# Loading the first chunk of x and the first quarter of w through the hardware DMA queues

## The chip, the cores and the metric

The kernel runs on one core of one Trainium2 chip. A core has a matrix engine (TensorE, PE in the profile, its weight loads PEld), a vector engine (VectorE, DVE), a scalar engine (ScalarE, ACT), a general engine (GpSimd, POOL) and a queue engine (SyncE, SP) that only issues DMAs. Data moves between device memory and the on-chip memory (SBUF) by 16 DMA engines. A DMA is issued on a queue: SyncE and ScalarE issue on hardware queues, which copy without a change of type; GpSimd issues on a software queue, which can cast float32 to bfloat16 on the way. The metric is the device time of the kernel in microseconds (us), the median of several runs.

## The reference

```python
B, S, D = (16, 2048, 1024)
def reference(x, w, decay):            # x [B,S,D], w [D,D], decay [D], float32
    xw = x @ w
    out[:, 0, :] = xw[:, 0, :]
    for t in range(1, S):
        out[:, t, :] = decay[None, :] * out[:, t - 1, :] + xw[:, t, :]
    return out
```

A matrix product, and along the time axis of each of its columns a decayed running sum.

## The kernel before

**Tiling.** The 32768 rows of x are cut into 64 chunks of 512 (`TL`). The inner dimension of 1024 is cut into four quadrants (`NQ`) of 256 (`CQ`); one contraction step k (8 of them, `K`) takes 32 of the 256 rows of each quadrant, so its 128 partitions are 4 blocks of 32. k = 2m + e with m in 0..3 and e in 0..1: the row of w that belongs to quadrant q, index i and step k is 256q + 64m + 2i + e, so the even and the odd rows of w belong to different e. An output block n (8 of them) is 128 columns of the result, laid on 128 partitions; blocks 0 to 3 (h = 0) are the first half of the columns, 4 to 7 (h = 1) the second. Matmuls are in bfloat16: `wsb` holds w, `xt` a chunk of x, transposed so that the contraction lies on partitions; the sum over k is made in PSUM.

**Steady state.** GpSimd's queue loads x casting to bfloat16 (`load`, L105), VectorE transposes blocks of 32 (`turn`, L115), ScalarE puts the pairs apart (`part`, L123), TensorE multiplies (`matmul`, L131), VectorE scans along time (`run` L233, `scan` L213), transposes back (`back`, L283) and SyncE stores (`store`, L306). A tile of the result is an instance of `Tile`.

**Order.** It is written out by hand. `pin` keeps every instruction in the order of the program on its engine. `agenda` is a table from a step to a string of deeds, a letter and a number each; `deeds` says which function a letter calls. Line -99 of the table is the opening, ahead of the first output tile. Each DMA takes one of eight completion semaphores of its kind (hardware or software) in turn, so that the ninth waits until the first of them has landed.

**The opening, which the change touches.** w is loaded in four parts (h, e), the "quarters", into `stage`, memory that later serves as output buffers (`room`); each part is 128 partitions of 4 sets (m) of 512 columns. `load_w` (L321) issues a part as four DMAs of one quadrant each (L323). `settle` (L328, copy on L330) copies one set m of a part to its place in `wsb`. x's first 256 rows come as float32 rows, 128 in each of two DMAs on the queues of SyncE and ScalarE (L341), into `whole`. `gather` (L376) casts them to bfloat16 into `upright`, `erect` (L386) transposes them on TensorE into PSUM (`bed`), `lay` (L393) copies them to `xt`. The second 256 rows come casting by `load_half` on GpSimd's queue and go through `turn` and `part` in halves; `begin(0)` multiplies the first half by all even k, `begin(1)` the second, 256 columns in each matmul. Then come the odd k of the whole chunk, which need w's second part (0, 1), then the first halves of chunk 1 and so on.

`spin` (L350) issues matmuls on a constant tile, whose result is not used; twelve of them open TensorE's work. `spin_on(q)` (L404) makes such matmuls wait for quadrant q of w's first part, by a copy of one of its columns into a `gate` tile. `identity(1)` makes the unit matrix for the transposes on GpSimd (L442, L443). `decays` (L424 to L430) turns the decay rows that SyncE loads on L356 into columns.

The letters of the opening: U = a part of w on GpSimd's queue; M = half a chunk of x on GpSimd's queue; I = unit matrix; H, J = `gather` on VectorE, ScalarE; t = `erect`; O, o = `lay` on ScalarE, VectorE; K = matmuls on the constant; W, w = `settle` of one set on VectorE, ScalarE; q, Q = the same for block 0 and for blocks 1 to 3; n = `begin`; E = a quarter of `turn`; F, G = a quarter of `part` on VectorE, ScalarE; D = `decays`; L = the next load of x. W0 to W3 are the sets of part (0, 0), q4 to W7 those of (0, 1), W8 to w15 those of h = 1.

Of the kernel before, what the change touches and what calls it, by code (L numbers as in the profile page):

```python
# [9 lines left out]
FP32 = mybir.dt.float32  # L10
BF16 = mybir.dt.bfloat16
# [3 lines left out]
def _ap(ap_obj: bass.AP, new_ap, extra_offset=0):  # L15
    return dataclasses.replace(
        ap_obj,
        ap=[list(p) for p in new_ap],
        offset=ap_obj.offset + extra_offset,
    )  # L20
# [5 lines left out]
def kernel(  # L26
# [26 lines left out]
    nc = tc.nc  # L53
    pin = tc.keep_in_program_order
    B, S, D = x.shape
    assert w.shape == (D, D)

    NQ = 4
    P = 32
    CQ = D // NQ  # L60
    K = CQ // P
    M = K // 2
    TL = 512
    NJ = TL // P
    NC = S // TL
    R = K // 2
    CH = D // 2
# [8 lines left out]
    def ring(pool, name, count, shape, dtype=FP32):  # L76
        i = turns[name] = turns.get(name, -1) + 1
        return pool.tile(shape, dtype, name=f"{name}{i % count}")

    def quad(q):  # L80
        return slice(q * P, (q + 1) * P)
# [59 lines left out]
    class Tile:  # L141
# [39 lines left out]
        def copy(self):  # L181
            self.xs = sb.tile([128, 2 * TL], FP32, name=f"xs{self.lot % 3}")[:, 0:self.T]
            parts = self.ps if isinstance(self.ps, tuple) else (self.ps,)
            size = self.T // len(parts)
            for i, ps in enumerate(parts):
                pin(nc.scalar.copy(out=self.xs[:, i * size:(i + 1) * size], in_=ps))  # L186
# [103 lines left out]
    class Outlet:  # L290
# [8 lines left out]
        def store(self, b, t0, j0, j1):  # L299
# [4 lines left out]
            for j in range(j0, j1, nj):  # L304
# [8 lines left out]

    room = [ot_tile(2 * NJ).rearrange("p j c -> p (j c)") for _ in range(2)]
    size = M * CH
    stage = {(0, 0): room[0][:, 0:size // 2].bitcast(BF16),
             (0, 1): room[0][:, size:size * 3 // 2].bitcast(BF16),
             (1, 0): room[1][:, 0:size // 2].bitcast(BF16),
             (1, 1): room[1][:, size // 2:size].bitcast(BF16)}

    def load_w(queues, h, e):  # L321
        for i, q in enumerate((0, 2, 1, 3)):
            pin(queues[i % len(queues)].dma_start(  # L323
                out=stage[h, e][quad(q)].rearrange("p (m d) -> p m d", m=M),
                in_=_ap(w, [[2 * D, P], [2 * P * D, M], [1, CH]],
                        (q * CQ + e) * D + h * CH)))

    def settle(h, e, m, copy):  # L328
        src = stage[h, e][:, m * CH:(m + 1) * CH]
# [4 lines left out]
    spare = ring(psp, "spare", 1, [128, TL])  # L334
    rows = const.tile([128, 2, P], FP32, name="rows")
    touch = const.tile([128, 1], BF16, name="touch")
    H = NJ // 2
    halves = ((0, H), (H, NJ))
    whole = room[1][:, size:2 * size].rearrange("p (u c) -> p u c", u=2)
    for u, queue in enumerate((nc.sync, nc.scalar)):  # L340
        pin(queue.dma_start(out=whole[:, u], in_=_ap(x, [[D, 128], [1, D]], u * 128 * D)))  # L341
    pin(nc.vector.memset(idle, 0.0))  # L342
    pin(nc.vector.memset(rows, 0.0))
    pin(nc.scalar.copy(out=touch, in_=idle[:, 0:1]))

    gates = [const.tile([128, 128], BF16, name=f"gate{q}") for q in range(NQ)]
    for gate in gates:
        pin(nc.vector.memset(gate, 0.0))

    def spin(count, by):  # L350
        for _ in range(count):
            pin(nc.tensor.matmul(out=spare, lhsT=by, rhs=idle, start=True, stop=True))  # L352

    spin(12, idle[:, 0:128])
    for q in range(NQ):
        pin(nc.sync.dma_start(  # L356
            out=rows[q * P:q * P + R],
# [3 lines left out]
    def load_half(i):  # L361
# [6 lines left out]
    seconds = [ps[:, TL:2 * TL] for ps in heads] + [spares[1]]  # L368
    eye = const.tile([128, 128], BF16, name="eye")

    upright = room[0][:, size * 3 // 2:2 * size].bitcast(BF16).rearrange(
        "p (e u m c) -> p e u m c", e=2, u=2, m=M)

    def gather(i, copy):
        e, u = i // 2, i % 2
        pin(copy(out=upright[:, e, u].rearrange("p m (q i) -> p m q i", q=NQ),  # L376
                 in_=whole[:, u].rearrange(
                     "p (q m i e) -> p e m q i", q=NQ, m=M, e=2)[:, e]))

    def bed(e):  # L380
        return seconds[e].bitcast(BF16).rearrange("p (m t) -> p m t", m=M)

    def erect(i):
        e, u = i // 2, i % 2
        for m in range(M):
            pin(nc.tensor.transpose(  # L386
                out=bed(e)[:, m, u * 128:(u + 1) * 128], in_=upright[:, e, u, m], identity=eye))

    def lay(i, copy):
        e, m = i // 2, i % 2 * 2  # L390
        if 0 not in xt_of:
            xt_of[0] = ring(sb, "xt", 5, [128, M, 2, TL], BF16)
        pin(copy(out=xt_of[0][:, m:m + 2, e, 0:H * P], in_=bed(e)[:, m:m + 2]))  # L393

    def begin(i):
        for k in range(0, K, 2):
            for n in range(R):
                if i == 0:
                    matmul(firsts[n], n, k, xt_of[0], 0, H * P)
                else:  # L400
                    matmul(firsts[n], n, k, xt_of[0], H * P, TL, pairs=xw_of[0])

    def spin_on(q):
        pin(nc.scalar.copy(out=gates[q][quad(q), 0:1], in_=stage[0, 0][quad(q), 0:1]))  # L404
        spin(3 if q == 0 else 2, gates[q])

    def load_part(i):
        load_w((nc.gpsimd,), i // 2, i % 2)

    def part_one(i, copy):  # L410
        part(i // 8, copy, i % 4, i % 4 + 1, *halves[i // 4 % 2])
# [106 lines left out]
    def turn_and_load(c):  # L518
# [19 lines left out]
        "E": lambda i: turn(i // 8, *halves[i // 4 % 2], i % 4, i % 4 + 1),  # L538
        "F": lambda i: part_one(i, nc.vector.tensor_copy),
        "G": lambda i: part_one(i, nc.scalar.copy),  # L540
        "K": spin_on,
        "t": erect,
        "H": lambda i: gather(i, nc.vector.tensor_copy),
        "J": lambda i: gather(i, nc.scalar.copy),
# [24 lines left out]
        "L": lambda i: load(*loads.pop(0)) if loads else None,  # L569
    }  # L570
    agenda = {
        -99: "U0 I1 M1 U1 M2 M3 U2 U3 H0 J1 t0 t1 H2 J3 t2 t3 O1 o0 K0 O3 o2 K2 K1 K3 W0 W1 w2 W3 n0 E4 E5 G4 E6 G5 E7 F6 G7 n1 q4 w5 Q4 W6 W7 D E8 E9 G8 E10 G9 E11 F10 G11 E12 L E13 G12 L E14 G13 E15 L F14 G15",
        0: "p0 z0 W8 W9 W10 W11",
        1: "g0",
        2: "L S1 L",
# [191 lines left out]
```

## Time and profile before

| | us |
|---|---|
| median of 3 runs (lowest, highest) | 903.61 (903.51, 903.97) |
| the profiled execution, its own time | 903.72 |
| its span, first to last instruction | 901.9 |
| TensorE busy | 891.2 |
| VectorE busy | 823.5 |
| ScalarE busy | 687.1 |
| GpSimd busy | 657.2 |

The profile is of one execution. The span is shorter than the time by what lies around the program. Busy times are sums over the span; an engine can be busy at something that nobody waits for. The chain of work that ended last is followed back from the last instruction, at each step to what released it; when it is read in order of time, a row is start, length, what. A row of the timeline is start, length, engine, line, operation, what is written and from what, how many; in brackets the idle time before it and what ended that. A row of a stretch is its two ends, its length, the busy time and number of instructions of TensorE, its weight loads, VectorE, ScalarE and GpSimd, the granted clock, the mean busy share of the 16 DMA engines and what they wrote in GB/s. A row of a DMA queue is its kind, packets, MB written, and the time of its packets as a share of 16 engines' time. TensorE's granted clock stands at 1.0 in every slice. All times in the text are from the start of the span.

### The profile page before, as it was taken

The page shows a single profiled execution, that of the slowest core. Times are in us where ns is not written, and L with a number is a line of the kernel's source. Part 1 is how long each engine was busy: PE and PEld are TensorE (multiplying, and loading weights), DVE is VectorE, ACT ScalarE, POOL GpSimd, SP SyncE. Part 2 cuts the span into 40 slices and gives each one's busy share as a digit, 9 for nine tenths or more (in the row PEclk, how much of TensorE's full clock was granted, in tenths as well). Part 3 has the DMA queues.
Part 4 walks back from the last instruction along what each step waited for, and adds up shares of the span by engine and source line. Part 5 has one row for each costly group of instructions (what it writes and reads, how often), then busy time and mean ns, then how long its engine had stood idle before and what let it go on. Part 6 is the DMA issues. An engine that isn't in the chain of part 4 may idle for free.

```text
span 901.9 us, 12229 instructions
## 1 busy us (share of the span) xinstructions
PE 891.2 (99%) x4131; PEld 411.9 (46%) x4213; DVE 823.5 (91%) x636; ACT 687.1 (76%) x962; POOL 657.2 (73%) x757
## 2 busy tenths in 40 slices
PE   8999999999999999999999999999999999999998
PEld 5544444444444444444444444444444444444444
DVE  4999998989999999999998999999999999999998
ACT  4889867778877877878778778777787787787743
POOL 8888678768767768677677687777777776876532
PEclk9999999999999999999999999999999999999999
DMA  9999999999999999999999999999999999999868
GB/s 193 195 215 218 229 212 207 216 233 247 247 248 255 248 255 252 246 254 250 222 235 228 218 236 227 233 226 227 232 230 227 227 236 222 226 228 221 177 153 231
DMA packets 402382, 204.77 MB, mean 227 GB/s; under 512 B 9360, under 2 KB 401552, under 8 KB 402320
## 3 DMA queue, kind: packets, MB, share of 16 engines
q1 hardware_dynamic: 265664, 134.77, 60.8%
q0 software_dynamic: 136512, 68.70, 56.8%
q8 instruction: 33, 0.54, 0.2%
q10 hardware_dynamic: 144, 0.52, 0.1%
q14 instruction: 29, 0.24, 0.1%
HBM read 138.42 MB, written 134.22 MB: 302 GB/s over the span
## 4 chain that ended last, share of the span: by engine, by line
PE 97%; DMA 1%; issue 1%; POOL 0%; DVE 0%; ACT 0%; DVEq 0%; POOLq 0%
PE ps L131 96%; PE spare L131 1%; DMA ot<-in_w_dram 1%; POOL ot L323 0%; DVE so L233 0%; PE ps L460 0%; PE spare L460 0%; ACT xb L467 0%; DVE wsb L419 0%; DVEq L419 0%; POOLq L751 0%
## 5 line engine op out<-in xcount | busy, mean ns | idle before, releaser
L131 PE MATMUL ps<-xt,wsb 128*128 128x512 bf16 (+1 forms) x3946 | 862.6, 378 | 4.7 <-DVE wsb L419 0.4
L131 PEld LDWEIGHTS <-wsb 128*128 128x128 bf16 x4160 | 406.5, 98 | 479.8 <-issue 0.9
L208 POOL TENSOR_TENSOR xs<-h,xs 128x512 f32<-128x512 f32 (+1 forms) x190 | 242.7, 1278 | 184.1 <-ACT h L169 83.1
L283 DVE STREAM_TRANSPOSE ot<-so 128x1024 f32<-128x1024 f32 (+2 forms) x265 | 300.2, 1171 | 6.5 <-DMA out_dram<-ot 4.4
L186 ACT COPY xs<-ps 128x1024 f32<-128x1024 f32 (+1 forms) x190 | 188.8, 994 | 149.3 <-PE ps L131 137.5
L266 POOL TENSOR_TENSOR so<-h,xs 128x512 f32<-128x512 f32 (+1 forms) x190 | 241.2, 1271 | 46.9 <-ACT h L169 27.2
L123 ACT COPY xt<-xw 128x2048 bf16<-128x2048 bf16 (+1 forms) x133 | 240.6, 1816 | 9.5 <-DVE xw L115 9.5
L105 POOL DMA_DIRECT2D xb<-in_x_dram x260 | 171.6, 661 | 2.9 <-DMA ot<-in_w_dram 0.9
L169 ACT ACTIVATE h<-so,dec 128x512 f32<-128x512 f32 (+1 forms) x190 | 145.3, 766 | 32.8 <-DVE so L213 29.9
L115 DVE STREAM_TRANSPOSE xw<-xb 128x2048 f32<-128x2048 f32 (+1 forms) x74 | 145.9, 1981 | 6.5 <-DMA xb<-in_x_dram 6.5
L213 DVE TENSOR_TENSOR_SCAN so<-spare,keep,xs 128x512 f32<-128x512 f32 (+1 forms) x97 | 119.8, 1237 | 25.9 <-POOL xs L208 25.6
L213 DVE TENSOR_TENSOR_SCAN so<-spare,xs 128x512 f32<-128x512 f32 x93 | 113.0, 1217 | 25.4 <-POOL xs L208 22.8
L169 ACT ACTIVATE h<-ps,dec 128x512 f32<-128x512 f32 (+1 forms) x189 | 129.3, 684 | 0.0
L233 DVE TENSOR_TENSOR_SCAN so<-dec,ps 128x1024 f32<-128x1024 f32 x34 | 76.9, 2260 | 0.8 <-ACT h L169 0.6
L233 DVE TENSOR_TENSOR_SCAN so<-dec,keep,ps 128x1024 f32<-128x1024 f32 (+2 forms) x35 | 74.7, 2138 | 0.0
L270 ACT COPY keep<-so 128x1 f32<-128x1 f32 x136 | 25.2, 188 | 9.1 <-DVE so L233 8.7
L204 ACT COPY so<-keep 128x1 f32<-128x1 f32 x97 | 18.4, 191 | 2.6 <-DVE ot L283 2.4
L131 PE MATMUL spare<-xt,wsb 128*128 128x512 bf16 (+1 forms) x68 | 14.0, 329 | 0.0
L323 POOL DMA_DIRECT2D ot<-in_w_dram x16 | 9.0, 561 | 2.9 <-POOLq L751 0.9
L202 POOL MEMSET so<- 128x1 f32 x93 | 10.7, 116 | 0.6 <-DVE ot L283 0.6
L131 PE MATMUL ps<-xw,wsb 128*128 128x256 bf16 (+1 forms) x56 | 9.3, 307 | 0.8 <-DVE xw L115 0.8
L352 PE MATMUL spare<-idle 128*128 128x512 bf16 x12 | 5.3, 632 | 1.2 <-DVE idle L342 1.2
(46 smaller groups left out, 43.9 us busy)
## 6 DMA issues: line engine op xcount, KB each, us to landing
out_dram<-ot SPq DMA_DIRECT2D x236, 512.0 KB, 10.8
xb<-in_x_dram POOLq DMA_DIRECT2D x248, 256.0 KB, 7.8
out_dram<-ot SPq DMA_DIRECT2D x56, 128.0 KB, 2.5
ot<-in_w_dram POOLq DMA_DIRECT2D x16, 128.0 KB, 5.6
out_dram<-ot SPq DMA_DIRECT2D x8, 256.0 KB, 4.2
xb<-in_x_dram POOLq DMA_DIRECT2D x12, 128.0 KB, 5.3
out_dram<-xb SPq DMA_DIRECT2D x4, 256.0 KB
ot<-in_x_dram ACTq DMA_DIRECT2D x1, 512.0 KB, 4.9
```

The lines of the kernel that those rows point to most:

```text
L105: pin(nc.gpsimd.dma_start(out=xb_of[c][quad(q), j0:j1], in_=_ap(x, [[D, P], [P * D, j1 - j0], [1, CQ]], (b * S + t0 + j0 * P) * D + q * CQ)))
L115: pin(nc.vector.transpose(out=dst.rearrange("p (m j i) -> p j m i", m=M, i=P)[:, j0:j1, m0:m1], in_=src.rearrange("p (j m c) -> p j m c", ...
L123: pin(copy(out=xt_of[c][:, m0:m1, :, j0 * P:j1 * P], in_=src))
L131: pin(nc.tensor.matmul(out=ps[:, t0:t1] if ps.shape[1] >= t1 else ps, lhsT=lhs, rhs=rhs, start=(k == 0 and t0 == start), stop=(k == K - 1),))
L169: pin(nc.scalar.activation(out=h, in_=src, func=mybir.ActivationFunctionType.Copy, scale=dec[:, self.n:self.n + 1]))
L186: pin(nc.scalar.copy(out=self.xs[:, i * size:(i + 1) * size], in_=ps))
L208: pin(nc.gpsimd.tensor_tensor(out=odds, in0=self.g, in1=odds, op=ALU.add))
L213: pin(nc.vector.tensor_tensor_scan(out=so[:, 3:T + 2:2], data0=squares[-1][:, n:n + 1].to_broadcast([128, T // 2]), data1=self.xs[:, 1:T:2 ...
L233: pin(nc.vector.tensor_tensor_scan(out=so[:, t + 2:t + 2 + size], data0=dec[:, n:n + 1].to_broadcast([128, size]), data1=ps, initial=befor ...
L266: pin(nc.gpsimd.tensor_tensor(out=self.so[:, 2:T + 2:2], in0=self.h, in1=self.xs[:, 0:T:2], op=ALU.add))
L270: pin(nc.scalar.copy(out=self.keep, in_=self.so[:, self.T + 1:self.T + 2]))
L283: pin(nc.vector.transpose(out=outlet.ot[:, j:j + size, c0:c0 + P], in_=self.so[:, t1:t1 + size * P].rearrange("p (i t) -> p i t", t=P)))
```

## The change

- x's first 512 rows, not 256, come as float32 rows of 4 KB, in four DMAs of 128 rows, two on SyncE's queue and two on ScalarE's. The second 256 rows land in chunk 0's own input buffer, `xb`. They too are cast, transposed on TensorE and copied to `xt`, as the first are.
- w's first quarter (0, 0) comes on the same two queues behind them, as float32, in four DMAs of one set each (`load_set`: 128 rows of 512 columns, one set m of all four quadrants). `settle` of this part is then a cast.
- GpSimd's queue loses w's first quarter and x's second half chunk. After the unit matrix GpSimd makes a copy of two elements for each partition out of x's first 256 rows (`hold`), and then issues w's second quarter and the rest as before.
- `begin(i)` now multiplies the whole chunk by k = 2i for the four blocks, 512 columns in each matmul, so that it needs set i alone.
- The gates go. Nine plain matmuls on the constant follow the first transposes, one the second.

```diff
--- before.py
+++ after.py
@@ -313,17 +313,18 @@
 
     room = [ot_tile(2 * NJ).rearrange("p j c -> p (j c)") for _ in range(2)]
     size = M * CH
-    stage = {(0, 0): room[0][:, 0:size // 2].bitcast(BF16),
+    stage = {(0, 0): room[0][:, 0:size],
              (0, 1): room[0][:, size:size * 3 // 2].bitcast(BF16),
              (1, 0): room[1][:, 0:size // 2].bitcast(BF16),
              (1, 1): room[1][:, size // 2:size].bitcast(BF16)}
 
-    def load_w(queues, h, e):
-        for i, q in enumerate((0, 2, 1, 3)):
-            pin(queues[i % len(queues)].dma_start(
-                out=stage[h, e][quad(q)].rearrange("p (m d) -> p m d", m=M),
-                in_=_ap(w, [[2 * D, P], [2 * P * D, M], [1, CH]],
-                        (q * CQ + e) * D + h * CH)))
+    def load_w(queue, h, e, m0=0, m1=M, quads=range(NQ)):
+        for q in quads:
+            pin(queue.dma_start(
+                out=stage[h, e][quad(q), m0 * CH:m1 * CH].rearrange(
+                    "p (m d) -> p m d", d=CH),
+                in_=_ap(w, [[2 * D, P], [2 * P * D, m1 - m0], [1, CH]],
+                        (q * CQ + e + 2 * P * m0) * D + h * CH)))
 
     def settle(h, e, m, copy):
         src = stage[h, e][:, m * CH:(m + 1) * CH]
@@ -334,24 +335,42 @@
     spare = ring(psp, "spare", 1, [128, TL])
     rows = const.tile([128, 2, P], FP32, name="rows")
     touch = const.tile([128, 1], BF16, name="touch")
+    held = const.tile([128, 2], FP32, name="held")
     H = NJ // 2
     halves = ((0, H), (H, NJ))
-    whole = room[1][:, size:2 * size].rearrange("p (u c) -> p u c", u=2)
-    for u, queue in enumerate((nc.sync, nc.scalar)):
-        pin(queue.dma_start(out=whole[:, u], in_=_ap(x, [[D, 128], [1, D]], u * 128 * D)))
+    xb_of[0] = ring(sb, "xb", 3, [128, NJ, CQ], BF16)
+    xw_of[0] = ring(sb, "xw", 2, [128, M, NJ, P, 2], BF16)
+    wholes = [room[1][:, size:2 * size],
+              xb_of[0].rearrange("p j c -> p (j c)").bitcast(FP32)]
+    wholes = [half.rearrange("p (u c) -> p u c", u=2) for half in wholes]
+
+    def load_rows(queue, i, u):
+        pin(queue.dma_start(
+            out=wholes[i][:, u], in_=_ap(x, [[D, 128], [1, D]], (2 * i + u) * 128 * D)))
+
+    def load_set(queue, e, m):
+        pin(queue.dma_start(
+            out=stage[0, e][:, m * CH:(m + 1) * CH],
+            in_=_ap(w, [[CQ * D, NQ], [2 * D, P], [1, CH]], (e + 2 * P * m) * D)))
+
+    load_rows(nc.sync, 0, 0)
+    load_rows(nc.scalar, 0, 1)
+    load_rows(nc.sync, 1, 0)
+    load_rows(nc.scalar, 1, 1)
+    load_set(nc.sync, 0, 0)
+    load_set(nc.scalar, 0, 1)
+    load_set(nc.sync, 0, 2)
+    load_set(nc.scalar, 0, 3)
     pin(nc.vector.memset(idle, 0.0))
     pin(nc.vector.memset(rows, 0.0))
     pin(nc.scalar.copy(out=touch, in_=idle[:, 0:1]))
 
-    gates = [const.tile([128, 128], BF16, name=f"gate{q}") for q in range(NQ)]
-    for gate in gates:
-        pin(nc.vector.memset(gate, 0.0))
-
-    def spin(count, by):
+    def spin(count):
         for _ in range(count):
-            pin(nc.tensor.matmul(out=spare, lhsT=by, rhs=idle, start=True, stop=True))
-
-    spin(12, idle[:, 0:128])
+            pin(nc.tensor.matmul(
+                out=spare, lhsT=idle[:, 0:128], rhs=idle, start=True, stop=True))
+
+    spin(12)
     for q in range(NQ):
         pin(nc.sync.dma_start(
             out=rows[q * P:q * P + R],
@@ -368,44 +387,41 @@
     seconds = [ps[:, TL:2 * TL] for ps in heads] + [spares[1]]
     eye = const.tile([128, 128], BF16, name="eye")
 
-    upright = room[0][:, size * 3 // 2:2 * size].bitcast(BF16).rearrange(
-        "p (e u m c) -> p e u m c", e=2, u=2, m=M)
+    upright = xw_of[0].rearrange("p m j i e -> p (m j i e)").rearrange(
+        "p (h e u m c) -> p h e u m c", h=2, e=2, u=2, m=M)
 
     def gather(i, copy):
-        e, u = i // 2, i % 2
-        pin(copy(out=upright[:, e, u].rearrange("p m (q i) -> p m q i", q=NQ),
-                 in_=whole[:, u].rearrange(
+        h, e, u = i // 4, i // 2 % 2, i % 2
+        pin(copy(out=upright[:, h, e, u].rearrange("p m (q i) -> p m q i", q=NQ),
+                 in_=wholes[h][:, u].rearrange(
                      "p (q m i e) -> p e m q i", q=NQ, m=M, e=2)[:, e]))
 
-    def bed(e):
-        return seconds[e].bitcast(BF16).rearrange("p (m t) -> p m t", m=M)
+    def bed(h, e):
+        return seconds[2 * h + e].bitcast(BF16).rearrange("p (m t) -> p m t", m=M)
 
     def erect(i):
-        e, u = i // 2, i % 2
+        h, e, u = i // 4, i // 2 % 2, i % 2
         for m in range(M):
             pin(nc.tensor.transpose(
-                out=bed(e)[:, m, u * 128:(u + 1) * 128], in_=upright[:, e, u, m], identity=eye))
+                out=bed(h, e)[:, m, u * 128:(u + 1) * 128],
+                in_=upright[:, h, e, u, m], identity=eye))
 
     def lay(i, copy):
-        e, m = i // 2, i % 2 * 2
+        h, e, m = i // 4, i // 2 % 2, i % 2 * 2
         if 0 not in xt_of:
             xt_of[0] = ring(sb, "xt", 5, [128, M, 2, TL], BF16)
-        pin(copy(out=xt_of[0][:, m:m + 2, e, 0:H * P], in_=bed(e)[:, m:m + 2]))
+        pin(copy(out=xt_of[0][:, m:m + 2, e, h * H * P:(h + 1) * H * P],
+                 in_=bed(h, e)[:, m:m + 2]))
 
     def begin(i):
-        for k in range(0, K, 2):
-            for n in range(R):
-                if i == 0:
-                    matmul(firsts[n], n, k, xt_of[0], 0, H * P)
-                else:
-                    matmul(firsts[n], n, k, xt_of[0], H * P, TL, pairs=xw_of[0])
-
-    def spin_on(q):
-        pin(nc.scalar.copy(out=gates[q][quad(q), 0:1], in_=stage[0, 0][quad(q), 0:1]))
-        spin(3 if q == 0 else 2, gates[q])
+        for n in range(R):
+            matmul(firsts[n], n, 2 * i, xt_of[0])
+
+    def hold(i):
+        pin(nc.gpsimd.tensor_copy(out=held, in_=wholes[0][:, :, 0:1].rearrange("p u c -> p (u c)")))
 
     def load_part(i):
-        load_w((nc.gpsimd,), i // 2, i % 2)
+        load_w(nc.gpsimd, i // 2, i % 2, quads=(0, 2, 1, 3))
 
     def part_one(i, copy):
         part(i // 8, copy, i % 4, i % 4 + 1, *halves[i // 4 % 2])
@@ -538,7 +554,8 @@
         "E": lambda i: turn(i // 8, *halves[i // 4 % 2], i % 4, i % 4 + 1),
         "F": lambda i: part_one(i, nc.vector.tensor_copy),
         "G": lambda i: part_one(i, nc.scalar.copy),
-        "K": spin_on,
+        "K": spin,
+        "v": hold,
         "t": erect,
         "H": lambda i: gather(i, nc.vector.tensor_copy),
         "J": lambda i: gather(i, nc.scalar.copy),
@@ -569,7 +586,7 @@
         "L": lambda i: load(*loads.pop(0)) if loads else None,
     }
     agenda = {
-        -99: "U0 I1 M1 U1 M2 M3 U2 U3 H0 J1 t0 t1 H2 J3 t2 t3 O1 o0 K0 O3 o2 K2 K1 K3 W0 W1 w2 W3 n0 E4 E5 G4 E6 G5 E7 F6 G7 n1 q4 w5 Q4 W6 W7 D E8 E9 G8 E10 G9 E11 F10 G11 E12 L E13 G12 L E14 G13 E15 L F14 G15",
+        -99: "I1 v U1 M2 M3 U2 U3 H0 J1 t0 t1 H2 J3 t2 t3 O1 o0 O3 o2 K9 H4 J5 t4 t5 H6 J7 t6 t7 o4 O5 K1 W0 n0 o6 w1 n1 W2 O7 n2 W3 n3 q4 w5 Q4 W6 W7 D E8 E9 G8 E10 G9 E11 F10 G11 E12 L E13 G12 L E14 G13 E15 L F14 G15",
         0: "p0 z0 W8 W9 W10 W11",
         1: "g0",
         2: "L S1 L",
```

## The prediction

> **What bounds the kernel now.** I read the page first: the busy table, then the chain of work that ended last.
>
> ```profile
> PE 891.2 (99%) x4131; PEld 411.9 (46%) x4213; DVE 823.5 (91%) x636; ACT 687.1 (76%) x962; POOL 657.2 (73%) x757
> ...
> PE 97%; DMA 1%; issue 1%; POOL 0%; DVE 0%; ACT 0%; DVEq 0%; POOLq 0%
> ```
>
> TensorE is busy for 99% of the span and makes up 97% of the chain. The change touches only the opening, so I read the chain in order of time there:
>
> ```profile
> 1.31 1.25 POOL ot L323 x2
> 2.56 5.65 DMA ot<-in_w_dram
> 8.21 0.28 issue
> 8.50 0.54 POOL ot L323
> 9.04 0.13 issue
> 9.16 5.43 DMA ot<-in_w_dram
> 14.60 0.03 issue
> 14.62 0.05 DVEq L419
> 14.67 0.04 issue
> 14.72 0.21 DVE wsb L419
> 14.92 0.05 issue
> 14.97 0.39 PE ps L131
> ```
>
> Until 14.97 us the chain is GpSimd's transfers of w's first two quarters. From 14.97 on it is matmuls with gaps of 0.05 us. So the end of the kernel moves by as much as the moment at which the odd-k matmuls of the first chunk begin; I call it Q, 14.97 now. Then I read the transfers of the first 30 us, and the rates by stretch (last two columns: DMA share, GB/s written).
>
> ```profile
> q0 software_dynamic: 7723, 4.74, 111.1%
> q1 hardware_dynamic: 192, 0.53, 5.9%
> q10 hardware_dynamic: 144, 0.52, 4.5%
> ```
> ```profile
> 3.00:4.00 1.00, 1.00 (x4) 0.33 (x3) 0.00 (x0) 0.00 (x0) 0.92 (x4) 1.00 1.05 430
> 4.00:5.00 1.00, 1.00 (x3) 0.30 (x2) 0.00 (x0) 0.00 (x0) 1.00 (x3) 1.00 1.01 384
> ...
> 14.00:15.00 1.00, 0.63 (x7) 0.31 (x4) 0.28 (x3) 0.56 (x2) 0.91 (x3) 1.00 1.44 193
> ```
>
> Float32 rows move at 430 GB/s on 16 DMA engines, 26.9 each. GpSimd's casting transfers write 193, so they read 386: 24.1 each. Queue q10 (ScalarE's) carried one transfer of 128 rows: 144 packets, 128 of data and 16 more. Queue q1 (SyncE's) carried an equal one and the four decay transfers: 192 - 144 = 48, 12 for each decay transfer. A decay transfer has 4 rows of two runs, so 8 packets of data and 4 more. Read as one closing packet for each engine that takes part, 128 rows go over 16 engines and a transfer whose outermost count is 4 over 4 engines, although it has 8 runs to share out. The split goes by the outermost count.
>
> **The change part by part.** *x's rows on the hardware queues.* The second 256 rows follow the first on the same queues. The rates by stretch (41, 197, 430, 384 GB/s from 1 to 5 us) add up to the first 1.05 MB at 5.0, and the casts begin at 5.43, 0.4 later. The second half, 1.05 MB at 430, takes 2.45: data in at 7.45, usable at about 7.9. ScalarE issues three more transfers of 0.41 ahead of its table load, 1.2 us, covered by its idle time up to 5.65.
>
> *w's first quarter by sets.* Four transfers of 128 rows of 2 KB, two on each hardware queue. Their source is written as 4 blocks of 32 rows, since each quadrant's rows lie 256 rows further on in w; the destination is 128 partitions. No row of before shows such a mixed transfer. The bounds are 16 engines, from the row transfer, and 4, from the decay transfers. I take 4: the decay transfers are the nearest row, the only ones here with 4 outermost, and they did not go on to split the second count. Each of the four engines then has 1.05 MB / 4 = 262 KB. At the middle of 24.1 and 26.9, 25.5 GB/s, this takes 10.3 us: from 7.45 to 17.7 if nothing else runs on them.
>
> The Trainium skill (page "DMA: Bandwidth & Descriptors", section "Why a DMA increments its semaphore by 16 and not by 1") states that the number of engines is the largest up to 16 that divides the slowest dimension of both sides, which gives 4 for 4 against 128. The packet counts above fit it for 4 against 4 and 128 against 128; no run here yet shows the mixed case, and by a rule that looked at the destination alone the sum would be the first rival's.
>
> *GpSimd's queue.* Eight transfers leave it (2.32 and 2.41 us of issue), and one small copy comes in that waits for the first x rows (5.65 at ScalarE). w's second quarter is issued from about 6.0 instead of 6.88. The first casting transfer, issued at 1.31, moved its first bytes at about 4.9, so I let this one begin at 9.0 (bounds 7.5 to 9.6). From then on the four engines serve three queues. Bounds for GpSimd's share there are none and one half; I take a third, the even split, since the three queues always have work. By 9.0 the sets have 40 KB of the 262; the other 222 at 17 GB/s take 13.0: data at 22.0, usable at 22.4. Sets 0 and 1 (131 KB per engine) land at 14.4 + 0.4 = 14.8, sets 2 and 3 at 22.4.
>
> *VectorE, ScalarE and TensorE up to the first real matmul.* The second half of chunk 0 now goes through gathers, sixteen transposes and four PSUM copies, instead of four VectorE transposes and four copies:
>
> ```profile
> 5.43 0.80 DVE L376 CAST ot<-ot 128x512 bf16<-128x512 f32 x2 [3.92 <-DMA ot<-in_x_dram]
> 5.65 1.21 ACT L376 CAST ot<-ot 128x512 bf16<-128x512 f32 x2 [2.98 <-DMA ot<-in_x_dram]
> 6.29 1.34 PE L386 MATMUL ps<-eye,ot 128*128 128x128 bf16 x16
> 7.23 0.58 ACT L393 COPY xt<-ps 128x512 bf16<-128x512 bf16 x1 [0.37 <-PE ps L386]
> 7.84 0.98 DVE L393 COPY xt<-ps 128x512 bf16<-128x512 bf16 x2 [1.62 <-ACT xt L393]
> ```
>
> The first transposes end at 7.63 as now (they wait for the 12 warming matmuls, which last to 6.29). Nine more at 0.215 end at 9.55; the new transposes follow. The first copy began 0.94 after the first transpose, so now at 10.5; at 0.56 between copies it ends at 11.05. The cast of set 0 (0.40, as in the first row) would follow, and the first real matmul start at 11.5. As set 0 lands at 14.8, all of this is hidden behind it. If the sets came in time, it would be on the path (first rival). The gate copies and memsets that go were hidden behind w's quads.
>
> *Matmuls of even k.* Sixteen of 512 columns take the place of 32 of 256, in four groups, one for each set. At the measured spacing 0.216 this is 3.46 us. Groups 0 and 1 run from 15.3. Set 2 is usable at 22.4; its cast (0.40) and the hand-over (0.05) give 22.85, and groups 2 and 3 take 1.73: Q = 24.6, 9.6 later than 14.97. VectorE's queue behind the waiting cast of set 2 holds set 3, w's second quarter, the decays and chunk 1's transposes; they are ready when needed: w's second quarter lands at about 17 (65 KB for each engine at 8.5 GB/s from 9.0), chunk 1's first half soon after 22.4, and Q + 3.46 is 28.1. The decay transfers stand behind the sets on SyncE's queue and are used after them.
>
> *TensorE's clock.* In the timeline the warming matmuls run at one in 0.43 us until about 6.6, after 5.4 us of work, then at 0.22. TensorE now stands idle from group 1 to 22.9, some 6 us (longest idle before, after the start: 0.8, with no loss). A second slow start costs between 0 and half of 5.4, 2.7. I take 2.2, nearer to the start's row, because the gap is nearer to a standing start than to 0.8.
>
> The Trainium skill (page "TensorE: Matmul & The Clock Gate", Part 1) puts the slow state after an idle window of about 3.4 us and the way back at as much work, from which I estimate 1.7, so 0.5 less than from the row.
>
> Sum: 9.6 + 2.2 = 11.8 us. The profiled execution took 903.72 (span 901.9 and 1.8 around it), 0.11 above the median 903.61, so 903.6 + 11.8 = 915.4. What follows Q runs as before: every load behind it is then earlier against TensorE.
>
> **The rivals.** *Not slower: the sets go over 16 engines.* The row transfers' 16 closing packets speak for it; the decay transfers' 4 speak against. Then 1.05 MB at 390 to 430 lands at 10.1 to 10.5, ahead of the casts, and the first real matmul starts at 11.5 by the working above: Q = 11.5 + 3.46 = 14.96 against 14.97. Time 903.6, from 903.2 (the nine warming matmuls or the copies 0.4 quicker) to 904.6 (GpSimd's stream delays sets 2 and 3 by 1 us). It decides from the point where the last set lands before about 12.8. Chance 0.16.
>
> *Four engines, and GpSimd's stream gives way.* In the old start nothing of GpSimd's moved while the hardware queues were full (until 4.7). Sets land at 17.7 + 0.4, Q = 18.1 + 0.45 + 1.73 = 20.3, 5.3 later, and 0 to 2.2 for the clock as the gap is only 3.4: 909 to 911. Chance 0.14.
>
> *Four engines, and it takes half.* 222 KB at 12.75 take 17.4: usable at 26.8, Q = 29.0, 14.0 later, with 2.2 makes 919.8. Chance 0.14.
>
> *Faster by over 0.2%* would need Q before 13.2, so a first real matmul at 9.7, about when the new transposes begin. Chance 0.03.
>
> *Another delay* (the waiting copy on GpSimd holding w's second quarter past 17, a missed late load): 906 to 909. Chance 0.03.
>
> **How the numbers follow.** My forecast, four engines with an even share, has 0.50; all of four engines 0.78, with its own range 908 to 921. This leaves more than 2 in 10 out, so the range takes in the 16 engines: 903 to 921. About 0.2% (1.8 us) is what a measurement of this kernel can tell from no change. Slower: 0.78, 0.03 and 0.01 of the first rival, 0.82. Within it: 0.15. Faster: 0.03.
>
> **What the profile after would show.** Right: hardware queues with 132 packets for each set (128 and 4); a DMA share near a quarter from hardware queues between 8 and 20 us; VectorE's cast of sets 2 and 3 waiting for a DMA of w until about 22; matmuls at 0.43 apart behind that wait; Q near 25 to 27, and no change after it. Wrong: 144 packets for a set, no wait of VectorE on w's sets, and matmuls from about 11.5 without a gap. It would also be wrong if Q moved but chunk 1's or w's later loads were the wait that ended last.

## The result and the profile after

| | before | after |
|---|---|---|
| median (lowest to highest) | 903.79 (903.51 to 904.04), 4 runs | 918.24 (917.05 to 918.87), 4 runs |
| the profiled execution, its own time | 903.72 | 918.34 |
| its span | 901.9 | 916.5 |
| mean granted clock | 1.000 | 0.991 |

The ratio is 1.0158, with a 95% interval of 1.0141 to 1.0176: the change makes the kernel 14.5 us slower. First the page of the changed kernel: busy time, the chain by engine, the granted clock in 40 slices, and the group of casts of w's sets.

```profile
PE 900.3 (98%) x4214; PEld 412.3 (45%) x4214; DVE 824.7 (90%) x631; ACT 687.4 (75%) x959; POOL 652.7 (71%) x750
...
PEclk7899999999999999999999999999999999999999
...
PE 97%; DMA 2%; SPq 0%; DVE 0%; issue 0%; ACT 0%
...
L331 DVE CAST wsb<-ot 128x512 bf16<-128x512 f32 x3 | 1.2, 424 | 13.3 <-DMA ot<-in_w_dram 13.3
```

Three casts of sets cost 1.2 us of work and 13.3 us of waiting for a DMA of w. DMA has gone from 1% to 2% of the chain, and the clock is no longer full in the first two slices of 22.9 us. Where in the span the loss sits is seen in the last copy of a PSUM tile on ScalarE, in the timeline of before and of after:

```profile
891.00 0.59 ACT L186 COPY xs<-ps 128x512 f32<-128x512 f32 x1 [1.82 <-PE ps L131]
```
```profile
905.51 0.59 ACT L186 COPY xs<-ps 128x512 f32<-128x512 f32 x1 [1.82 <-PE ps L131]
```

It is 14.5 later. Counted off one by one, the copies from about 130 us of before on stand 14.5 later than their partners there, but for six (five between 196 and 213 us, one at 506) that stand 13.1 to 14.4 later; the next ones are at 14.5 again. So nothing lasting is lost or won in the steady state; all of the loss is in the opening. There the chain of after, in order of time (start, length, what), reads:

```profile
1.66 0.71 SPq L352
2.37 0.05 issue
2.42 22.65 DMA ot<-in_w_dram
25.07 0.02 issue
25.09 0.44 DVE wsb L331
25.53 0.05 issue
25.58 1.46 PE ps L131 x3
```

L352 is the issue of a set on SyncE's queue. The chain no longer goes through GpSimd: from 2.42 to 25.07 it is one transfer of w on a hardware queue, then the cast of set 2, then matmuls. The timeline shows all four sets, w's second quarter and the odd k (bracket: idle before, and what ended it):

```profile
17.90 0.43 DVE L331 CAST wsb<-ot 128x512 bf16<-128x512 f32 x1 [6.89 <-DMA ot<-in_w_dram]
18.38 1.46 PE L131 MATMUL ps<-xt,wsb 128*128 128x512 bf16 x3 [7.07 <-DVE wsb L331]
...
22.21 0.62 ACT L331 COPY wsb<-ot 128x512 bf16<-128x512 bf16 x1 [2.84 <-DMA ot<-in_w_dram]
...
25.09 0.76 DVE L331 CAST wsb<-ot 128x512 bf16<-128x512 f32 x2 [6.43 <-DMA ot<-in_w_dram]
...
25.58 1.46 PE L131 MATMUL ps<-xt,wsb 128*128 128x512 bf16 x3 [3.60 <-DVE wsb L331]
...
28.96 1.32 PE L131 MATMUL ps<-xt,wsb 128*128 128x512 bf16 x3
```

Set 0 is usable at 17.90, sets 2 and 3 at 25.09, w's second quarter at 22.21, ahead of its need. The last row is Q: 28.96, 13.99 later than 14.97. TensorE stood for 7.07 and again for 3.60 us. The clock by stretch (the third number from the end) shows the price:

```profile
10.00:12.00 2.00, 1.17 (x13) 0.73 (x13) 0.42 (x1) 1.23 (x3) 0.80 (x2) 1.00 1.20 200
12.00:14.00 2.00, 0.00 (x0) 0.00 (x0) 0.00 (x0) 0.00 (x0) 0.00 (x0) 0.73 1.29 192
14.00:16.00 2.00, 0.00 (x0) 0.00 (x0) 0.00 (x0) 0.00 (x0) 0.00 (x0) 0.50 0.86 125
...
28.00:30.00 2.00, 2.00 (x6) 0.76 (x5) 1.27 (x4) 1.66 (x3) 1.63 (x4) 0.50 1.12 157
30.00:32.00 2.00, 2.00 (x11) 0.88 (x9) 1.73 (x5) 1.26 (x3) 1.78 (x4) 1.00 1.14 184
```

The trace's clock records put the ends of the half-speed stretch at 12.92 and 29.99. They begin only at 6.10 us (6.88 in before); ahead of that the rows show 1.00 for want of a record, though the warming matmuls stand 0.43 us apart, at half speed. Groups 2 and 3 take 3.38 us instead of 1.73, so 1.65 too long, and the first 1.03 us after Q cost 0.51 more. Q's shift and this 0.51 make 14.5, the whole of the loss. The DMA queues of the first 30 us (packets, MB, share):

```profile
q0 software_dynamic: 3086, 1.88, 48.6%
q1 hardware_dynamic: 600, 1.58, 16.4%
q10 hardware_dynamic: 552, 1.57, 15.2%
```

On ScalarE's queue 552 packets are two row transfers of 144 and two sets of 132; SyncE's 600 are the same and 48 for the decays. So each set has four closing packets, as if it went over four engines, like a decay transfer.

### The profile page after: what moved, and what is told of

Its sections match the earlier page's. It is cut to its first block, busy times and chain, and to the rows that moved or that the text cites. A ratio compares the mean times of both kernels' runs of the same rounds, so it can differ in the third digit from the quotient of the medians.

```text
span 916.5 us, 12301 instructions
## 1 busy us (share of the span) xinstructions
PE 900.3 (98%) x4214; PEld 412.3 (45%) x4214; DVE 824.7 (90%) x631; ACT 687.4 (75%) x959; POOL 652.7 (71%) x750
## 4 chain that ended last, share of the span: by engine, by line
PE 97%; DMA 2%; SPq 0%; DVE 0%; issue 0%; ACT 0%
PE ps L131 95%; DMA ot<-in_w_dram 2%; PE spare L131 1%; DVE so L233 0%; SPq L348 0%; SPq L352 0%; PE ps L476 0%; DVE wsb L331 0%; PE spare L476 0%; ACT xb L483 0%
## 5 line engine op out<-in xcount | busy, mean ns | idle before, releaser
L131 PE MATMUL ps<-xt,wsb 128*128 128x512 bf16 x4028 | 871.5, 379 | 10.7 <-DVE wsb L331 10.7
L105 POOL DMA_DIRECT2D xb<-in_x_dram x256 | 169.1, 661 | 11.5 <-DMA ot<-in_w_dram 9.9
L270 ACT COPY keep<-so 128x1 f32<-128x1 f32 x136 | 25.5, 190 | 8.9 <-DVE so L233 8.6
L331 DVE CAST wsb<-ot 128x512 bf16<-128x512 f32 x3 | 1.2, 424 | 13.3 <-DMA ot<-in_w_dram 13.3
L323 POOL DMA_DIRECT2D ot<-in_w_dram x12 | 6.8, 567 | 3.8 <-DMA xb<-in_x_dram 3.1
L370 PE MATMUL spare<-idle 128*128 128x512 bf16 x22 | 7.7, 511 | 1.2 <-DVE idle L364 1.2
```

What stands on the lines that cost most here:

```text
L105: pin(nc.gpsimd.dma_start(out=xb_of[c][quad(q), j0:j1], in_=_ap(x, [[D, P], [P * D, j1 - j0], [1, CQ]], (b * S + t0 + j0 * P) * D + q * CQ)))
L131: pin(nc.tensor.matmul(out=ps[:, t0:t1] if ps.shape[1] >= t1 else ps, lhsT=lhs, rhs=rhs, start=(k == 0 and t0 == start), stop=(k == K - 1),))
L270: pin(nc.scalar.copy(out=self.keep, in_=self.so[:, self.T + 1:self.T + 2]))
```

## The experiments

The theory: the sets move on 4 of the 16 engines because the outermost count of their source is 4, and two costs come on top: what GpSimd's stream takes of those four engines, and a second slow start of TensorE's clock. The rivals: that the two hardware queues cannot bring x and w in time on any number of engines; that GpSimd's stream alone is the cause; that the new path of x (casts, transposes, copies) is. The diffs are against the changed kernel. Before was run again beside them and took 903.83 (903.52 to 904.15, 7 runs; e1 to e4) and 903.56 (903.30 to 904.25, 13 runs; e5 to e8).

### e1: the same bytes as blocks of 32 rows

```diff
-    load_set(nc.sync, 0, 0)
-    load_set(nc.scalar, 0, 1)
-    load_set(nc.sync, 0, 2)
-    load_set(nc.scalar, 0, 3)
+    load_w(nc.sync, 0, 0, quads=(0, 2))
+    load_w(nc.scalar, 0, 0, quads=(1, 3))
```

> Only the cut of w's first quarter changes: the same 1.05 MB on the same two hardware queues, as four quadrants of 32 rows with four runs of 2 KB each, instead of four sets of 128 rows. Outermost counts are then 32 and 32. Theory (the number of DMA engines goes by the outermost count of the source, 4 in the set transfers): each transfer runs on 16 engines, 128 packets of data and 16 closing ones, so ScalarE's queue shows 576 packets and not 552; all four land at 10.5 to 11.5, the casts no longer wait, the odd-k matmuls begin at 15.0 to 15.5, time 903.6 to 904.5. Rival A (three queues share the engines, whatever their number; float32 w on the hardware queues is late for that): the last cast still waits past 17 and the time stays over 908. Rival B (rows of 2 KB are slow on the hardware queues): as rival A.

Measured: 909.02 (908.27 to 909.10), ratio 1.0056 (1.0039 to 1.0073). It wins back 9.2 of the 14.5 us, but is not the 904 that was expected. The queue has the packets of 16 engines (576 = 4 times 144), yet the sets are usable only from 13.35 on, in the timeline:

```profile
13.35 0.43 DVE L331 CAST wsb<-ot 128x512 bf16<-128x512 f32 x1 [3.00 <-DMA ot<-in_w_dram]
```

The stretches show why (last two numbers: DMA share, GB/s written):

```profile
7.00:8.00 1.00, 1.00 (x10) 0.53 (x8) 0.50 (x2) 0.90 (x2) 1.00 (x3) 1.00 0.99 375
8.00:9.00 1.00, 1.00 (x6) 0.43 (x5) 1.00 (x3) 0.22 (x1) 1.00 (x2) 1.00 0.97 231
9.00:10.00 1.00, 0.92 (x13) 0.66 (x11) 0.12 (x2) 0.99 (x2) 1.00 (x3) 1.00 0.95 227
```

Rows of x to 128 partitions move at 375 to 430 GB/s; from 8 us, when the transfers of one quadrant each (the quads), to 32 partitions, follow, all engines are still busy and the rate is 227 to 254. TensorE idles 3.39 us, its clock is half from 12.87 to 19.70, so Q is 20.18 where a first matmul at 13.83 would give 17.29 at full clock: 2.3 of the 5.2 us is the landing, 2.9 the clock. Thus 16 engines in this shape do not bring the time of before back. Whether the shape or GpSimd's stream slowed them is left to e8.

### e2: sets of 128 rows with one outermost count of 128

```diff
-            in_=_ap(w, [[CQ * D, NQ], [2 * D, P], [1, CH]], (e + 2 * P * m) * D)))
+            in_=_ap(w, [[2 * D, NQ * P], [1, CH]], (e + 2 * P * m) * D)))
```

As many bytes in rows as long, to the same 128 partitions; only the rows taken are others of w.

> The set transfers keep their number, size, queues and runs of 2 KB, but read 128 rows in one even step, so that the source's outermost count is 128. The rows are not those that belong to the set: the product is of another w, and only the time is read. Theory: 16 engines, 144 packets for each set (576 on ScalarE's queue), sets 0 and 1 land at 8.5 to 9.5 and sets 2 and 3 at 10.5 to 11.5, no wait of VectorE on a set after 11.5, first real matmul at 11.5, time 903.3 to 904.3. Rivals A and B: sets 2 and 3 past 17, time over 908.

Measured: 904.62 (one run; 903.72 for the profiled execution of before). 144 packets for each set, and no loss of clock. In the timeline:

```profile
11.31 0.82 PE L131 MATMUL ps<-xt,wsb 128*128 128x512 bf16 x3 [1.08 <-DVE wsb L331]
12.71 0.76 DVE L331 CAST wsb<-ot 128x512 bf16<-128x512 f32 x2 [1.12 <-DMA ot<-in_w_dram]
...
15.54 0.36 DVE L435 COPY wsb<-ot 128x128 bf16<-128x128 bf16 x2 [2.08 <-DMA ot<-in_w_dram]
15.80 0.82 PE L131 MATMUL ps<-xt,wsb 128*128 128x512 bf16 x3 [0.70 <-DVE wsb L435]
```

The first real matmul begins at 11.31, against the 11.5 that the first rival of the prediction worked out for its case. Sets 2 and 3 are usable at 12.71, not at 10.5 to 11.5, and the time is a little over the 903.3 to 904.3 that were expected; but against the 918.34 of the changed kernel, an outermost count of 128 instead of 4 is worth 13.7 us. The 0.8 that stays is a new wait: Q is 15.80 because w's second quarter, issued by GpSimd at 6.24, lands last.

### e3: eight blocks of 16 rows

```diff
-            in_=_ap(w, [[CQ * D, NQ], [2 * D, P], [1, CH]], (e + 2 * P * m) * D)))
+            in_=_ap(w, [[CQ * D // 2, 2 * NQ], [2 * D, P // 2], [1, CH]], (e + P * (m % 2)) * D)))
```

Again only the source differs, and other rows of w are taken.

> The set transfers read 8 blocks of 16 rows instead of 4 blocks of 32 (rows of w that don't belong to the set; only the time is read). Theory: 8 engines, 136 packets for each set (560 on ScalarE's queue); each engine has 64 packets of the sets in place of 128, so the sets' stretch of 17.6 us (7.4 to 25.1) falls to about half or less: sets 2 and 3 usable at 13.5 to 16.5, time 904.5 to 908. If the count did not matter, 918; if the source's second dimension were split as well, 904 as with 16 engines.

Measured: 909.02 (one run). The queue shows 560 packets, 136 for each set: 8 engines. The chain:

```profile
2.47 15.48 DMA ot<-in_w_dram
17.97 0.44 DVE wsb L331
18.45 0.82 PE ps L131 x3
```

Sets 2 and 3 are usable at 17.97, later than the 13.5 to 16.5 expected and between 25.09 (4 engines) and 12.71 (16). From 4 over 8 to 16 engines the time goes 918.2, 909.0, 904.6: the time follows the number of engines, and through it the outermost count of one side. Both edits also read other rows of w, and no run keeps the count and changes the rows alone; but the closing packets change with the count, 132, 136, 144.

### e4: GpSimd silent until sets 1 and 2 have landed

```diff
-        pin(nc.gpsimd.tensor_copy(out=held, in_=wholes[0][:, :, 0:1].rearrange("p u c -> p (u c)")))
+        pin(nc.gpsimd.tensor_copy(out=held, in_=stage[0, 0][:, 2 * CH - 1:4 * CH - 1:CH]))
```

> GpSimd's small copy waits for w's sets 1 and 2 instead of x's first rows, so that nothing of GpSimd's queue runs beside the sets. Theory with contention on the four engines: alone, 128 packets of 84 to 96 ns (the durations in the changed kernel's trace) take 10.8 to 12.3 us from 7.45: sets 2 and 3 usable at 18.6 to 20.2 instead of 25.1. But w's second quarter is issued only then and is the next wait: issued at about 19.5, usable at 25 to 26.5, odd k begin there, time 914 to 917. If the four engines were slow by themselves and GpSimd's stream cost nothing: sets still at 25, and the second quarter at 31, time 921 to 924.

Measured: 918.4 (one run), a little over the expected. Its stretches, while only the sets move:

```profile
10.00:12.00 2.00, 0.94 (x12) 0.73 (x13) 0.42 (x1) 1.08 (x2) 0.00 (x0) 1.00 0.26 100
12.00:14.00 2.00, 0.00 (x0) 0.00 (x0) 0.12 (x1) 0.00 (x0) 0.00 (x0) 1.00 0.26 100
```

A DMA share of 0.26 is 4.2 of 16 engines, and 100 GB/s is 25 for each of four. This is the disputed cost by itself. And its chain:

```profile
2.41 16.56 DMA ot<-in_w_dram
...
19.71 1.78 POOL ot L323 x3
21.49 5.64 DMA ot<-in_w_dram
...
27.26 0.21 DVE wsb L435
```

Without GpSimd's stream sets 2 and 3 are usable at 18.99, so the stream cost them 25.09 - 18.99 = 6.1 us in the changed kernel. What is won there is lost again by w's second quarter, which now comes last, at 27.26; Q is 27.51, and a half-speed clock until 31.68 adds 2.1. So GpSimd's stream beside the sets is not what the loss needs: four engines alone, with the second quarter after them, cost as much.

### e5: TensorE kept busy

Matmuls on the constant tile fill the two waits: 31 instead of 1 after the second transposes, and 21 more, into another PSUM bank, between groups 1 and 2.

```diff
-... t6 t7 o4 O5 K1 W0 n0 o6 w1 n1 W2 O7 n2 W3 n3 ...
+... t6 t7 o4 O5 K31 W0 n0 o6 w1 n1 W2 O7 i21 n2 W3 n3 ...
```

> The changed kernel with matmuls on the constant through its two waits: 31 instead of 1 before the first real matmul, 21 between the groups of sets 1 and 2 (into the second spare PSUM bank). The waits for w's sets stay as they are. Theory (the idle time put TensorE at half clock, and that cost the rest of the loss): granted clock 1.0 throughout, groups 2 and 3 in 1.73 us instead of 3.38 and the odd-k matmuls in 3.46 instead of 3.97, so 2.2 us less: 916.0 against 918.2. Rival (the matmuls there were slow because of the DMA traffic or the waits on weights): still 0.43 apart, 918 to 918.5.

Measured: 916.54 (916.33 to 916.77), ratio 1.0142 (1.0127 to 1.0157): 1.7 less than the change's median. The clock holds (mean 0.999), in the chain:

```profile
24.64 0.44 DVE wsb L331
25.13 0.82 PE ps L131 x3
25.95 0.22 PE spare L131
26.17 0.65 PE ps L131 x3
```

Groups 2 and 3 take 1.73 us (25.13 to 26.87). The last copy stands here at:

```profile
902.90 0.59 ACT L186 COPY xs<-ps 128x512 f32<-128x512 f32 x1 [1.82 <-PE ps L131]
```

This is 2.61 earlier than in after. The sets landed 0.45 earlier in this execution, so 2.16 is the clock, as counted above. The whole time shows less of it because the last stores took 1.1 us longer in this execution; why is open.

### e6: e2 with GpSimd silent

Both edits, that of e2 and that of e4.

```diff
-            in_=_ap(w, [[CQ * D, NQ], [2 * D, P], [1, CH]], (e + 2 * P * m) * D)))
+            in_=_ap(w, [[2 * D, NQ * P], [1, CH]], (e + 2 * P * m) * D)))
...
-        pin(nc.gpsimd.tensor_copy(out=held, in_=wholes[0][:, :, 0:1].rearrange("p u c -> p (u c)")))
+        pin(nc.gpsimd.tensor_copy(out=held, in_=stage[0, 0][:, 2 * CH - 1:4 * CH - 1:CH]))
```

> As the run with 128 even rows in each set (16 engines; not the set's rows, so another product), but GpSimd's small copy waits for sets 1 and 2, so that GpSimd issues nothing while they load. Theory (GpSimd's issuing slows the hardware queues: in that run they moved 100 packets of 2 KB per 0.5 us at 8.0 and 30 to 35 between 9.0 and 11.0, while nothing of GpSimd's had yet moved): sets 2 and 3 usable at 10.3 to 10.9 instead of 12.7, then w's second quarter, issued at about 10.9, usable at 16 to 18, the odd k begin there, time 905 to 907.5. Rival (rows of w come slowly for themselves on 16 engines): sets 2 and 3 again at 12.5 or later, time over 907.

Measured: 910.47 (one run). Sets 2 and 3 are usable at 11.56, against 12.71 in e2 and 10.3 to 10.9 expected: the part of e2's lateness that goes away with GpSimd silent is 1.1 us, and the rest stays. The stretches, with GpSimd still (its busy time is the fifth):

```profile
8.00:9.00 1.00, 1.00 (x7) 0.41 (x6) 0.92 (x3) 0.73 (x3) 0.00 (x0) 1.00 1.09 375
9.00:10.00 1.00, 1.00 (x17) 0.88 (x16) 0.32 (x2) 0.55 (x1) 0.00 (x0) 1.00 1.09 262
```

The rate falls from 375 to 262 between 9 and 10 us although the engines stay busy. The reason is open. In e2, while GpSimd issued, it fell to 129 and 131 from 9 to 11 us with engines 0.60 and 0.75 busy, before GpSimd's first packet moved at 11.37: so it is not GpSimd's data that slowed the sets there. The time is not the 905 to 907.5 expected but worse than e2's by 5.8, since w's second quarter is issued at 12.28 and usable only at 19.88, with a half-speed clock from 16.34 to 23.17. w's second quarter must not wait for the first.

### e7: x's rows alone

w's first quarter goes back to GpSimd, ahead of the unit matrix; x's second half stays on the hardware queues.

```diff
-    stage = {(0, 0): room[0][:, 0:size],
+    stage = {(0, 0): room[0][:, 0:size // 2].bitcast(BF16),
...
-    load_set(nc.sync, 0, 0)
-    load_set(nc.scalar, 0, 1)
-    load_set(nc.sync, 0, 2)
-    load_set(nc.scalar, 0, 3)
...
-        -99: "I1 v U1 M2 ...
+        -99: "U0 I1 U1 M2 ...
```

> The half of the change that concerns x: its 512 rows on the hardware queues, with the new path to xt and the matmuls by sets; w's first quarter stays on GpSimd's queue, casting, issued first as before, and nothing waits on GpSimd. Theory (the loss is all in the set transfers; and GpSimd's stream starts when the hardware queues are drained, at about 7.8): w's first quarter usable at 11 to 11.5, the second at 14.3 to 15, odd k from 15.0 to 15.4, time 903.6 to 904.3. Rival (the new path to xt or the matmuls by sets carry a loss of their own): 905 or more.

Measured: 903.80 (903.50 to 904.49, 10 runs), ratio 1.0002 (0.9993 to 1.0012): no difference. Its Q is 15.24, 0.27 later than before. In the timeline the first settle of w still waits for its DMA:

```profile
11.43 0.29 DVE L331 COPY wsb<-ot 128x512 bf16<-128x512 bf16 x1 [1.06 <-DMA ot<-in_w_dram]
```

So the casts, sixteen transposes and copies of x's second half, in place of its casting load, cost nothing that can be measured. All of the 14.5 belongs to w's sets.

### e8: both of w's first quarters as blocks of 32 rows on hardware queues

```diff
-             (0, 1): room[0][:, size:size * 3 // 2].bitcast(BF16),
+             (0, 1): room[0][:, size:2 * size],
...
+    load_w(nc.sync, 0, 0, quads=(0, 2))
+    load_w(nc.scalar, 0, 0, quads=(1, 3))
+    load_w(nc.sync, 0, 1)
...
-        pin(nc.gpsimd.tensor_copy(out=held, in_=wholes[0][:, :, 0:1].rearrange("p u c -> p (u c)")))
+        pin(nc.gpsimd.tensor_copy(out=held, in_=stage[0, 0][:, 0:2]))
...
-        -99: "I1 v U1 M2 ... K9 ... K1 ...
+        -99: "I1 v M2 ... K4 ... K3 ...
```

> A version meant to gain: x's 512 rows, w's first and second quarter all on the hardware queues as float32, w by quadrants of 32 rows (16 engines), the second quarter's four on SyncE's queue alone; GpSimd issues nothing until the first quarter has landed; 4 matmuls on the constant instead of 9 after the first transposes and 3 instead of 1 after the second. 4.2 MB at about 410 GB/s from 2.0: w's first quarter usable at 10.5, the second at 12.8, first real matmul at 11.0, odd k from 14.4 (14.97 before), chunk 1's first half at about 16: 903.0 to 903.5. If the hardware queues move rows of w at no more than 250 GB/s whatever GpSimd does, the first quarter comes at 12 and the second at 16.5: odd k from 16.8, and over 905.5.

Measured: 907.65 (907.18 to 907.80), ratio 1.0043 (1.0026 to 1.0059). GpSimd moves nothing until the first quarter is in, and the rate is still (stretches):

```profile
7.00:8.00 1.00, 1.00 (x14) 0.82 (x12) 0.01 (x1) 0.65 (x3) 0.00 (x0) 1.00 1.01 389
8.00:9.00 1.00, 0.65 (x3) 0.10 (x1) 0.94 (x3) 0.62 (x2) 0.00 (x0) 1.00 1.07 225
9.00:10.00 1.00, 0.71 (x12) 0.67 (x12) 0.59 (x3) 1.00 (x2) 0.00 (x0) 1.00 1.05 217
```

So e1's slowness was not GpSimd's stream: w's float32 rows into 32 partitions at a time move at 209 to 254 GB/s with all engines busy. In e6, with GpSimd as silent, w's rows to 128 partitions at a time moved at 375 from 8 to 9 us, against 225 here, though at 262 in the next us. A quad also has four runs for each partition where a set has one; which of the two slows it is open. The gain that was meant (903.0 to 903.5) did not come. The other case of the expectation did, and later than it said: sets are usable at 13.57, w's second quarter at 18.00. Both ways of loading w in blocks on 16 engines are thus slower than before, and no run gave a kernel faster than before.

## Why the prediction was right

918.2 lies within the range (903 to 921) and within the forecast's own range (908 to 921); the side and the four engines are the forecast's; that the size came near is in part luck, as said below. The sum, 11.8, is 2.8 under the 14.6 of the profiled execution.

- *Four engines for a set.* Right: 132 packets each, 25 GB/s for each engine alone (e4; 25.5 taken), and the order of 4, 8 and 16 (e3, e2). The Trainium skill (page "DMA: Bandwidth & Descriptors", section "Why a DMA increments its semaphore by 16 and not by 1") has the number of engines as the largest up to 16 that divides the slowest counts of both sides. The trace agrees for the mixed case, which before could not show: 4 against 128 gave 132 packets, 8 against 128 gave 136, 128 against 128 gave 144. A rule that looked at the destination alone would have given 16 engines each time.
- *The last landing: the step that was mis-sized.* Taken: sets 2 and 3 usable at 22.4; measured: 25.09, so 2.7 more, nearly all of the 2.8. 0.9 of it is the time without GpSimd's stream: usable at 18.99 (e4) and not at 18.1, since x's last rows were late (their last packet moved at 8.37 in the changed kernel, where all were taken to be in at 7.45). The other 1.8 is GpSimd's stream, which cost 6.1 (25.09 - 18.99) where 4.3 was taken (22.4 - 18.1). The even third was not the mechanism. From 10 to 16 us the hardware queues moved (packets, MB, share), first in the changed kernel, then in e4 without GpSimd:

```profile
q1 hardware_dynamic: 68, 0.14, 11.4%
q10 hardware_dynamic: 70, 0.14, 11.3%
```
```profile
q1 hardware_dynamic: 153, 0.31, 13.1%
q10 hardware_dynamic: 151, 0.30, 13.0%
```

This is 138 against 304, so GpSimd's stream cost over half for these 6 us, as the rival of a half had it. From 8 to 10 us it was 93 packets of some 101, so next to nothing, although GpSimd's first packet had moved at 8.10, and from 16 to 23 us 243 of some 355, a third. Set 0 came at 17.90 for this, and not at 14.8; that did not count, since sets 2 and 3 were still to come. Over the whole, from 8.10 to the last packet at 24.94, the sets moved at 15.1 GB/s for each engine, 0.60 of the 25 that they have alone. That the average cost, 40%, lies nearer to the third than to the half is luck; the landing came nearer to the 26.8 of the rival than to 22.4, and the time nearer to its 919.8 than to 915.4.

- *What GpSimd's stream consists of.* The prediction named w's second quarter alone against the sets and let it land at 17, yet took a third up to 22. GpSimd also issues the first eight loads of chunk 1's x behind it (from 8.50), so the stream does go on, past the second quarter's landing at 22.21 and up to the sets' end.
- *Cast and hand-over.* 0.49 measured (25.09 to 25.58), 0.45 taken. Even k without the clock: 1.73 for two groups (e5), as taken.
- *The clock.* 1.65 + 0.51 = 2.16 by the changed kernel's own matmuls, 2.16 by e5; 2.2 taken from the row of the start. That the size came out is in part luck. The prediction let the clock fall in the wait behind group 1; the trace has the fall at 12.92, in the 7.07 us ahead of set 0, a wait that the prediction had left out of the clock's account. Groups 0 and 1 then ran at half speed too, hidden by the wait for set 2. And the price differs with the moment at which the clock comes back: half the time from the first matmul behind the wait to that moment is 1.5 in e6 (20.14 to 23.17), 2.1 in e4 and 2.9 in e1. The Trainium skill (page "TensorE: Matmul & The Clock Gate", Part 1), from which 1.7 was estimated, has windows of 3.41 us that run freely, whenever the work begins. The spacing in the records agrees with that: in after the clock changes at 12.92 and 29.99, 17.07 apart, five windows; in e1 at 12.87 and 19.70, two. Matmuls had run for 4.41 us at half speed when the last change came, so the way back took more than one window's work. The estimate had left out where in the window the work begins. The idle window of about 3.4 us that the prediction set ahead of a fall was not needed in full: the fall came 1.6 us after the last matmul had ended in after (11.31 to 12.92), 2.4 in e1 (10.44 to 12.87).
- *Cover that held.* The longer path of x (e7: 0.27 later at Q, nothing in the time), SyncE's and ScalarE's extra issues, and w's second quarter, though it came at 22.21 where about 17 was taken. x's second half was usable at 8.50 and 9.45, not 7.9; the sets hid that too.
- *The rival of 16 engines* was right about its own case: e2 gave 904.6, the upper end of its 903.2 to 904.6, and a load behind GpSimd's queue is what it waits for. But the wait that ended last is that for w's second quarter, and not, as the rival had it, that for sets 2 and 3.
- *No effect behind Q.* Right: 14.5 at the last copy, as, but for six, at those from about 130 us on.

Open remain the slowing of the 128-row sets after 9 us with GpSimd silent (e6), what in the shape of a quad slows it (e1, e8), and the longer last stores in e5.

## What to carry to other kernels

Before a load is written as blocks, look at the outermost counts of both sides of its access pattern, and count the closing packets of a like transfer in the profile: an outer 4 here meant 4 of 16 engines, 100 GB/s instead of 375 to 430, and with what followed from it 14.5 us. Once a few engines carry the load that ends a wait, any other stream that visits those engines lengthens it, so ask what else will be in flight and for how long. A long wait of the matrix engine can cost more than its length: here 2.2 us of 14.5 was the clock, and matmuls on a constant gave it back (e5). Waits of 2.9 us and more (the shortest in e8) brought the clock down in these runs, those of up to 1.7 us (e4) did not.

## What the runs showed of the hardware

- Float32 rows of 2 KB that go to 32 partitions in one transfer moved at 209 to 254 GB/s with all 16 engines busy (e1, e8), against 375 to 430 for rows of x of 4 KB to 128 partitions, and 375 for rows of w of 2 KB to 128 partitions from 8 to 9 us (e6). By the median of each us, a packet of 2 KB took 117 to 173 ns there, 84 in e6.
- A casting transfer of GpSimd's moved its first packet 1.4 us after the issue when the hardware queues were empty (e4: 19.71 to 21.13, e6: 12.28 to 13.71), 1.9 when these held only 4-engine transfers behind x's last rows (after: 6.19 to 8.10), and over 5 when transfers for all 16 engines were queued (e1: 6.13 to 11.56, e2: 6.24 to 11.37).
- On engines that GpSimd's stream also used, the sets' 2 KB packets took 115 to 219 ns from 10 to 16 us in the changed kernel, by the median of each us and queue, and 84 to 96 from 16 us on, where they came less often than alone; alone 84 (e4).
- The falls and rises of TensorE's clock in the opening lay whole multiples of 3.41 us apart: 3.41 (e3, e8), 6.83 (e1, e6), 17.07 (after).
